# FoX's background weight work in half steps, with loads and stores a step apart from their uses

## The chip, the cores and the metric

The kernel runs on one core of one Trainium2 chip. The metric is the device time of one execution in microseconds (us). Its engines are named as in the profile: PE (TensorE matmul), PEld (its weight load), DVE (VectorE), ACT (ScalarE), POOL (GpSimd) and SP (SyncE, which issues nearly all DMAs, in order, and waits for each one's semaphores before it).

## The reference

One decoder layer on a sequence of 2048 tokens of width 1024, float32:

```python
shift_a, scale_a, gate_a, shift_m, scale_m, gate_m = split(silu(c) @ w_ada + b_ada, 6)
h = rms_norm(x, g_attn) * (1 + scale_a) + shift_a
q_f, k_f, v_f, q_s, k_s, v_s, f_logit = split(h @ w_in)
o_fox = forgetting_attention(q_f, k_f, v_f, log_sigmoid(f_logit + b))   # 8 heads, causal softmax
o_sb = stick_breaking_attention(q_s, k_s, v_s)                          # 8 heads, causal
mix = concat(head_rms_norm(o_fox, g_out_fox), head_rms_norm(o_sb, g_out_sb))
x = x + gate_a * (mix @ w_out)
h = rms_norm(x, g_mlp) * (1 + scale_m) + shift_m
u_gate, u_val = split(causal_conv3(h @ w_up))
x = x + gate_m * ((silu(u_gate) * u_val) @ w_down)
out = rms_norm(x, g_final)
```

The forgetting attention adds F[t] - F[s] to the logits, where F is the running sum of log f. c is one vector, so the six modulation vectors are one row each: gate_a and gate_m are wanted as a row that stands on all 128 partitions, shift_m and scale_m as columns.

## The kernel before

Every matmul operand is split into a high and a low part, and a product takes three matmuls. Attention is cut into 32 units: stick-breaking pairs of heads 0 to 3, then FoX pairs 0 to 3, each in four blocks of 512 tokens (tb 0 to 3). Units 16 to 31 are FoX; a unit has 6, 14, 22 or 30 groups of key tiles for tb 0 to 3. While `attend` (L596) goes through the groups of a unit, `fill_proj` puts steps of the next unit's projection between them: `proj` (L334) loads the eight tiles of h of a block from DRAM (`hp<-hs`, L339, 512 KB each), multiplies them for q, keeps them for k and, in every second pair, for v. A pair's q and k are rearranged through L285 and L295, its weights loaded at L246.

`late_mod` (L633) is work that nothing in attention needs: it hides in the FoX units. It makes the four remaining modulation vectors, parts 2 (gate_a), 5 (gate_m), 3 and 4, from eight loads of w_ada each (`hp<-in_w_ada_dram`, L654, 512 KB): ACT multiplies each half by a column of silu(c) (L660), POOL adds it to the sum `wsum` (L661). For gate_a, `fold_out` (L621) then multiplies w_out by g_out_fox and gate_a, splits the result (ACT at L44, POOL at L45) and stores it to `wos` (L631); its loads are L624. Both are generators; the main loop (L849) takes four steps of them in each of the units 17 to 30, whatever the unit's length.

One ring of ten buffers of 4 KB a partition, `h_tile()`, serves it all: the h tiles, the w_ada and w_out loads, the sums, the gate row, the folded weights. `wide()` is the same ring seen as one row:

```python
    def h_tile():
        return sl_.tile([P, 2, TB], F32R, name="hp", bufs=10)
    def wide():
        return f(h_tile()).rearrange("p a n -> p (a n)")
```

At the entry of a pair's first block (`enter_unit`, L777) all eight rows of F (`Fb<-fs`, L786: four blocks by two heads, 256 KB each) are loaded into a ring of eight that the pair before still reads (DVE at L514, POOL at L509).

The order on each engine is not the program's: a scheduler places every instruction as early as its simulated times and the free buffers let it, in-order engines then keep that order on the chip. An instruction that waits there holds all that stand behind it on its engine, SP's DMAs too.

## Time and profile before

| | before |
|---|---|
| median of 3 runs | 3091.8 us (3090.09 to 3096.59) |
| profiled execution, its own time | 3091.86 us |
| its span, first to last instruction | 3089.7 us |
| busy PE, PEld, DVE, ACT, POOL | 95%, 81%, 67%, 53%, 40% of the span |
| granted clock of PE, mean | 0.987 |
| HBM read, written | 352.61 MB, 90.51 MB |

Busy is a share of the span in which at least one instruction of the engine ran. PEclk is the granted share of the full clock: 1.00 is 2.4 GHz, 0.50 is 1.2 GHz. Stick-breaking lasts to about 850 us, FoX to about 1565 us, then come the output projection and, from about 1740 us, the channel mixer.

### The profile page before, as it was taken

Reading aid. Unit: us, or ns where it says so; the run is one execution under the profiler, and the core shown is the slowest. Engines: PE = TensorE matmul, PEld = TensorE weight load, DVE = VectorE, ACT = ScalarE, POOL = GpSimd, SP = SyncE. Lnnn points to the kernel's source line nnn. Section 1 sums busy time; section 2 is a strip of 40 time slices with the busy share of each in tenths; the row PEclk is TensorE's granted clock in tenths of the full one; section 3 lists DMA queues with packets and bytes.
Section 4 is the critical chain, followed back from the end, with each engine's and each line's share of the span. In section 5 each row is a group of like instructions: output and inputs, shape, how many; then the busy total and the mean of one; then the engine's idle time right before and its main releaser. Section 6 shows DMA issues by size and latency. Waiting matters only on the chain.

```text
span 3089.7 us, 46285 instructions
## 1 busy us (share of the span) xinstructions
PE 2945.4 (95%) x15934; PEld 2500.0 (81%) x15934; DVE 2080.9 (67%) x3416; ACT 1647.1 (53%) x3033; POOL 1228.0 (40%) x1459
## 2 busy tenths in 40 slices
PE   6899899999999999998989899999899999999998
PEld 5778798988788788987878688888678888888887
DVE  6686788878856675657733677778987777254253
ACT  5575777777765655566734544444544444343332
POOL 2673655556531332342122344444444443332331
PEclk8999999999999999999999999999999999999999
DMA  9457634565166865595457532223322223665562
GB/s 272 157 165 257 194 114 148 180 199 163 30 221 216 289 214 183 169 330 133 160 187 231 186 99 82 82 82 89 113 87 84 86 84 113 197 198 166 184 204 79
DMA packets 292811, 496.51 MB, mean 161 GB/s; under 512 B 29336, under 2 KB 177552, under 8 KB 291552
## 3 DMA queue, kind: packets, MB, share of 16 engines
q1 hardware_dynamic: 280944, 480.92, 49.4%
q10 hardware_dynamic: 11632, 12.63, 1.2%
q8 instruction: 126, 2.06, 0.3%
q14 instruction: 109, 0.89, 0.1%
HBM read 352.61 MB, written 90.51 MB: 143 GB/s over the span
## 4 chain that ended last, share of the span: by engine, by line
PE 58%; DVE 11%; DMA 10%; POOL 8%; issue 6%; ACT 4%; SPq 1%; POOLq 0%; DVEq 0%; ACTq 0%
PE ps_pj L271 8%; PE ps_o L1158 8%; PE ps_o L985 7%; PE ps_pv L401 6%; PE ps_pt L386 5%; PE ps_pj L313 5%; PE ps_t L1158 4%; PE ps_bc L1158 4%; PE ps_qk L371 3%; DMA wuraw<-in_w_up_dram 3%; PE ps_qk L372 3%; PE ps_t L985 2%; DMA hp<-hs 2%; DVE wu L45 2%; PE ps_o L738 1%
## 5 line engine op out<-in xcount | busy, mean ns | idle before, releaser
L985 PE MATMUL ps_o<-oa,wu 128*128 128x512 f32 x2088 | 503.3, 392 | 14.9 <-ACT oa L44 6.8
L985 PEld LDWEIGHTS ps_o<-oa,wu 128*128 128x128 f32 x2088 | 390.3, 188 | 105.2 <-DVE oa L45 9.8
L401 PE MATMUL ps_pv<-at,V 128*128 128x256 f32 x2304 | 432.9, 298 | 14.0 <-ACT at L390 6.0
L391 DVE TENSOR_TENSOR at<-ps_pt,at 128x512 fp32r<-128x512 f32 (+1 forms) x576 | 365.8, 653 | 117.2 <-ACT at L390 114.6
L271 PE MATMUL ps_pj<-hp,w_qk 128*128 128x512 f32 x1512 | 413.0, 405 | 28.0 <-DMA hp<-hs 13.4
L390 ACT ACTIVATE at<-ps_pt 128x512 fp32r<-128x512 f32 (+1 forms) x576 | 319.5, 580 | 169.0 <-PE ps_pt L386 126.6
L401 PEld LDWEIGHTS ps_pv<-at,V 128*128 128x128 f32 x2304 | 340.1, 191 | 48.2 <-DVE at L391 13.9
L475 POOL TENSOR_TENSOR a<-a,rw 128x512 f32<-128x512 f32 (+2 forms) x272 | 260.8, 962 | 234.8 <-DVE rw L470 98.6
L271 PEld LDWEIGHTS ps_pj<-hp,w_qk 128*128 128x128 f32 x1512 | 273.8, 190 | 86.8 <-DMA hp<-hs 17.0
L45 DVE TENSOR_TENSOR wd<-wide,wd 128x1024 fp32r<-128x1024 f32 x88 | 117.3, 1340 | 248.8 <-ACT wd L44 244.4
L371 PE MATMUL ps_qk<-K,Q 128*128 128x512 f32 (+2 forms) x640 | 257.5, 404 | 11.0 <-DMA K<-q 5.0
L45 POOL TENSOR_TENSOR g<-graw,g 128x512 fp32r<-128x512 f32 x82 | 141.3, 1726 | 294.8 <-ACT g L44 291.8
L1158 PE MATMUL ps_o<-wd,g 128*128 128x512 f32 x1040 | 249.3, 389 | 0.1
L985 PE MATMUL ps_t<-ob,wu 128*128 128x512 f32 x984 | 241.5, 390 | 0.7 <-ACT hf_m L884 0.7
L372 PE MATMUL ps_qk<-K,Q 128*128 128x512 f32 (+2 forms) x640 | 235.1, 368 | 0.0
L313 PE MATMUL ps_pj<-w_v,hp 128*128 128x256 f32 (+1 forms) x1536 | 229.9, 291 | 4.8 <-DVE zn L319 3.7
L44 ACT ACTIVATE wu<-wuraw 128x512 fp32r<-128x512 f32 x214 | 133.1, 626 | 183.4 <-PE ps_o L985 113.9
L470 DVE TENSOR_TENSOR_SCAN rw<-rw,ps_edge 128x512 f32<-128x512 f32 x168 | 211.8, 1271 | 26.1 <-ACT rw L460 25.0
L1158 PEld LDWEIGHTS ps_o<-wd,g 128*128 128x128 f32 x1040 | 195.2, 188 | 41.1 <-DVE y L1104 0.5
L985 PEld LDWEIGHTS ps_t<-ob,wu 128*128 128x128 f32 x984 | 184.7, 188 | 40.2 <-ACT hf_m L884 1.1
L313 PEld LDWEIGHTS ps_pj<-w_v,hp 128*128 128x128 f32 x1536 | 206.7, 193 | 12.9 <-issue 4.3
L386 PE MATMUL ps_pt<-edge,a 128*128 128x128 f32 x1088 | 182.3, 275 | 15.2 <-DVE at L391 8.9
(221 smaller groups left out, 5697.7 us busy)
## 6 DMA issues: line engine op xcount, KB each, us to landing
hp<-hs SPq DMA_DIRECT2D x224, 512.0 KB
wuraw<-in_w_up_dram SPq DMA_DIRECT2D x84, 512.0 KB
wide<-in_w_down_dram SPq DMA_DIRECT2D x84, 512.0 KB
Q<-q SPq DMA_DIRECT2D x128, 256.0 KB
g<-u SPq DMA_DIRECT2D x42, 512.0 KB
graw<-g SPq DMA_DIRECT2D x82, 256.0 KB
hs<-hp SPq DMA_DIRECT2D x32, 512.0 KB
K<-q SPq DMA_DIRECT2D x128, 128.0 KB
```

The lines of the kernel that those rows point to most:

```text
L45: (lo_engine or nc.gpsimd).tensor_sub(lo, src, f(hi))
L271: nc.tensor.matmul(acc, w[kt][:, a, n], h[:, bb], start=kt == 0 and i == 0, stop=kt == KT - 1 and i == 2)
L313: nc.tensor.matmul(av[:, t * width:(t + 1) * width], hts[kt][:, a, tok], w[1][kt][:, bb, 0:width], start=kt == 0 and m == 0, stop=kt == KT ...
L371: nc.tensor.matmul(b[:, :cw], Q[:, hl, 0, qcols], K[:, hl, :cw], start=True, stop=False)
L372: nc.tensor.matmul(b[:, :cw], Q[:, hl, 1, qcols], K[:, hl, :cw], start=False, stop=True)
L386: nc.tensor.transpose(b[:, i * P:(i + 1) * P], self.blk(self.kts[kk], qi), ident)
L390: nc.scalar.activation(at[:, 0, lo:], b[:, lo:], AF.Copy)
L391: nc.vector.tensor_sub(at[:, 1, lo:], b[:, lo:], f(at[:, 0, lo:]))
L401: nc.tensor.matmul(o[:, 0:2 * P], head.V[kt // 4][:, kt % 4, head.hl, :], rhs, start=self.first and kk == 0 and w == 0, stop=self.last and ...
L475: nc.gpsimd.tensor_mul(a[:, :need], a[:, :need], r[:, 1:need + 1])
L985: nc.tensor.matmul(b, w[:, p, j], o[:, q], start=first and i == 0, stop=last and i == 2, skip_group_check=True)
L1158: nc.tensor.matmul(banks[t][n], g[:, a, t * P:(t + 1) * P], w[:, b, n * TB:(n + 1) * TB], start=k == 0 and i == 0, stop=k == NKD - 1 and i ...
```

## The change

A step of the late work now handles one half row (256 KB) instead of a whole one, and 118 of them are spread evenly over the groups of units 17 to 30 (`pace`). A part's loads of w_ada all use one ring buffer `w`, whose two halves alternate: a step issues the load for the next step, then multiplies and adds its own half. The sum has a pool of its own (`late`) and also takes the gate row. `fold_out` works in place in one ring buffer; load, work and store stand in different steps, and its loads and stores are pinned behind what was issued before them on SP (`keep_in_program_order`). The rows of F are loaded block by block: blocks 0 and 1 at a pair's first unit, block 2 at its second, block 3 at its third. The instructions of PE, DVE, ACT and POOL are the same in kind and number; SP issues 64 loads of w_ada instead of 32 and 16 of w_out instead of 8.

```diff
--- before.py
+++ after.py
@@ -82,6 +82,7 @@
     mod_a = const.tile([P, 2, KT], F32, name="mod_a")
     mod_m = const.tile([P, 2, KT], F32, name="mod_m")
     bf_c = const.tile([4 * NH, 1], F32, name="bf_c")
+    LATE_STEPS = 118
     R_GA, R_GM, R_GF, R_GS, R_BA = 0, 8, 16, 20, 24
 
     def rms_scale(pool, xts, tag, junk=None):
@@ -619,17 +620,24 @@
             yield unit
 
     def fold_out(gt):
-        for kt in range(KT):
-            raw = wide()
-            nc.sync.dma_start(raw, w_out[kt * P:(kt + 1) * P, :])
-            for n in range(2):
-                sl = slice(n * TB, (n + 1) * TB)
-                nc.vector.scalar_tensor_tensor(raw[:, sl], raw[:, sl], cols[:, R_GF + kt:R_GF + kt + 1], gt[:, sl],
-                                               ALU.mult, ALU.mult)
-                w = h_tile()
-                split(w[:, 0], w[:, 1], raw[:, n * TB:(n + 1) * TB])
-                nc.sync.dma_start(wos[kt][:, :, n * TB:(n + 1) * TB], f(w))
-                yield
+        halves = [(kt, slice(n * TB, (n + 1) * TB)) for kt in range(KT) for n in range(2)]
+
+        def load(kt, sl):
+            w = h_tile()
+            tc.keep_in_program_order(nc.sync.dma_start(f(w)[:, 1], w_out[kt * P:(kt + 1) * P, sl]))
+            return w
+
+        w = load(*halves[0])
+        yield
+        for k, (kt, sl) in enumerate(halves):
+            raw = f(w)[:, 1]
+            nc.vector.scalar_tensor_tensor(raw, raw, cols[:, R_GF + kt:R_GF + kt + 1], gt[:, sl], ALU.mult, ALU.mult)
+            split(w[:, 0], w[:, 1], raw)
+            yield
+            tc.keep_in_program_order(nc.sync.dma_start(wos[kt][:, :, sl], f(w)))
+            if k + 1 < len(halves):
+                w = load(*halves[k + 1])
+            yield
 
     def late_mod():
         cr = f(h_tile())[0:2 * NFULL + 1].rearrange("p a (b n) -> p (a b) n", b=4)[:, 0:4]
@@ -648,30 +656,38 @@
         yield
         late = ((2, 0), (5, 1), (3, None), (4, None))
         for part, gate in late:
-            wsum = wide()
-            for kt in range(KT):
-                w = wide()
-                nc.sync.dma_start(w, w_ada[kt * P:(kt + 1) * P, part * D:(part + 1) * D])
-                for n in range(0, D, 512):
-                    sl = slice(n, n + 512)
-                    if kt == 0:
-                        nc.gpsimd.tensor_scalar_mul(wsum[:, sl], w[:, sl], cs[:, 0:1])
-                    else:
-                        nc.scalar.activation(w[:, sl], w[:, sl], AF.Copy, scale=cs[:, kt:kt + 1])
-                        nc.gpsimd.tensor_add(wsum[:, sl], wsum[:, sl], w[:, sl])
+            wsum = lp.tile([P, D], F32, name="wsum", bufs=1)
+            w = wide()
+
+            def load(k):
+                n = k % 2 * TB
+                nc.sync.dma_start(w[:, n:n + TB], w_ada[k // 2 * P:(k // 2 + 1) * P, part * D + n:part * D + n + TB])
+
+            load(0)
+            yield
+            for k in range(2 * KT):
+                kt, sl = k // 2, slice(k % 2 * TB, (k % 2 + 1) * TB)
+                if k + 1 < 2 * KT:
+                    load(k + 1)
+                if kt == 0:
+                    nc.gpsimd.tensor_scalar_mul(wsum[:, sl], w[:, sl], cs[:, 0:1])
+                else:
+                    nc.scalar.activation(w[:, sl], w[:, sl], AF.Copy, scale=cs[:, kt:kt + 1])
+                    nc.gpsimd.tensor_add(wsum[:, sl], wsum[:, sl], w[:, sl])
                 yield
             if gate is not None:
-                gt = wide()
-                nc.sync.dma_start(gt, b_ada[0:1, part * D:(part + 1) * D].to_broadcast([P, D]))
+                nc.sync.dma_start(w, b_ada[0:1, part * D:(part + 1) * D].to_broadcast([P, D]))
+                yield
                 for n in range(2):
+                    sl = slice(n * TB, (n + 1) * TB)
                     b = pt()
-                    nc.tensor.matmul(b, ones, wsum[:, n * 512:(n + 1) * 512], start=True, stop=True)
-                    nc.vector.tensor_add(gt[:, n * 512:(n + 1) * 512], b, gt[:, n * 512:(n + 1) * 512])
+                    nc.tensor.matmul(b, ones, wsum[:, sl], start=True, stop=True)
+                    nc.vector.tensor_add(wsum[:, sl], b, w[:, sl])
                     yield
                 if gate == 0:
-                    yield from fold_out(gt)
+                    yield from fold_out(wsum)
                 else:
-                    nc.sync.dma_start(gate_m, gt)
+                    nc.sync.dma_start(gate_m, wsum)
             else:
                 cb = pt()
                 for d in range(KT):
@@ -779,17 +795,17 @@
         while made[0] <= u.index:
             taken_before = taken[0]
             fill_proj(taken_before + 1)
-        if u.kind == "fox" and u.tb == 0:
-            Fbs[u.p] = [[sx.tile([P, TB], F32, name="Fb", bufs=8) for _ in range(NTB)] for _ in range(2)]
-            for t in range(NTB):
+        if u.kind == "fox":
+            for t in ((0, 1), (2,), (3,), ())[u.tb]:
                 for h in range(2):
-                    nc.sync.dma_start(Fbs[u.p][h][t],
-                                      fs[2 * u.p + h:2 * u.p + h + 1, t * TB:(t + 1) * TB].to_broadcast([P, TB]))
+                    b = sx.tile([P, TB], F32, name="Fb", bufs=8)
+                    nc.sync.dma_start(b, fs[2 * u.p + h:2 * u.p + h + 1, t * TB:(t + 1) * TB].to_broadcast([P, TB]))
+                    Fbs.setdefault(u.p, ([], []))[h].append(b)
         if u.index >= len(units) - 2:
             head_scale(u.index - len(units) + 2, pt(), sx)
         if u.index == len(units) - 1:
             drain(lm)
-            close_pool("sl", "psa")
+            close_pool("late", "sl", "psa")
             psc = open_pool("psc", side="right", space=PSUM)
             p2a = open_pool("p2a")
             tail = first_mix([load_o(0, p) for p in range(3)])
@@ -843,9 +859,10 @@
     ex = edge_bank = None
     psa = open_pool("psa", side="right", space=PSUM)
     sx = open_pool("fx", side="right")
+    lp = open_pool("late", side="right")
     base = taken[0]
     seen = {}
-    late = {}
+    pace = [0.0]
     for u in attend(plan[16:], 2, 2):
         seen[u.index] = seen.get(u.index, 0) + 1
         share = seen[u.index] / u.count
@@ -853,8 +870,9 @@
         if tail is not None:
             next(tail, None)
         elif u.index > 16:
-            while late.get(u.index, 0) < min(4, 4 * share):
-                late[u.index] = late.get(u.index, 0) + 1
+            pace[0] += LATE_STEPS / sum(v.count for v in plan[17:31])
+            while pace[0] >= 1:
+                pace[0] -= 1
                 next(lm, None)
     drain(tail)
     drain(first_out())
```

What the scheduler makes of it, at three places. A tile of h is named hs_k_n: k is its place among the eight, and n runs from 60 to 67 for block 0, 68 to 75 for block 1, 76 to 83 for block 2 and 84 to 91 for block 3.

SP, while gate_a is folded into w_out and pair 1 of FoX begins. Before:

```order
L786 DMA Fb<-fs 128x512 x4
L624 DMA hp<-in_w_out_dram 128x1024
L631 DMA wos_184<-hp 256x1x512
L339 DMA hp<-hs_0_76 128x1024
L295 DMA K<-q_13099 64x512 x4
L631 DMA wos_185<-hp 256x1x512
L339 DMA hp<-hs_1_77 128x1024
L624 DMA hp<-in_w_out_dram 128x1024
L786 DMA Fb<-fs 128x512
L631 DMA wos_185<-hp 256x1x512
L786 DMA Fb<-fs 128x512 x2
L339 DMA hp<-hs_2_78 128x1024
```

Now, at the same stage:

```order
L802 DMA Fb<-fs 128x512 x4
L637 DMA wos_185<-hp 256x1x512
L627 DMA hp<-in_w_out_dram 128x512
L340 DMA hp<-hs_2_70 128x1024
L340 DMA hp<-hs_3_71 128x1024
L340 DMA hp<-hs_4_72 128x1024
L340 DMA hp<-hs_5_73 128x1024
L340 DMA hp<-hs_6_74 128x1024
L340 DMA hp<-hs_7_75 128x1024
L340 DMA hp<-hs_0_76 128x1024
L340 DMA hp<-hs_1_77 128x1024
```

The tiles of block 2 stood one by one between rows of F, stores of folded weights and rearranged q and k; now the rows of F come first, and the tiles of block 1 and the first two of block 2 follow each other.

ACT, in the sum of gate_m (before at L660, now at L675), among attention's copies (L390, now L391) and exponentials (L519, now L520). Before:

```order
L660 ACTIVATE hp<-hp,cs 128x512 x2
L390 ACTIVATE at<-ps_pt 128x512
L390 ACTIVATE at<-ps_pt 128x384
L519 ACTIVATE p,ls<-p,mn 128x1792
L281 ACTIVATE q_15311<-ps_pj 128x512
L660 ACTIVATE hp<-hp,cs 128x512 x2
L390 ACTIVATE at<-ps_pt 128x512 x2
L424 ACTIVATE o_14681<-ps_pv 64x256
L390 ACTIVATE at<-ps_pt 128x512
L44 ACTIVATE q_15312<-ps_pj 128x512
L519 ACTIVATE p,ls<-p,mn 128x1920
```

Now:

```order
L675 ACTIVATE hp<-hp,cs 128x512
L391 ACTIVATE at<-ps_pt 128x512 x2
L675 ACTIVATE hp<-hp,cs 128x512
L425 ACTIVATE o_14689<-ps_pv 64x256
L391 ACTIVATE at<-ps_pt 128x512
L520 ACTIVATE p,ls<-p,mn 128x1920
L675 ACTIVATE hp<-hp,cs 128x512
L44 ACTIVATE V<-ps_pj 128x4x64
L675 ACTIVATE hp<-hp,cs 128x512
L391 ACTIVATE at<-ps_pt 128x512 x2
L44 ACTIVATE V<-ps_pj 128x4x64
```

Two halves of one load stood side by side; now they stand apart, and each has a load of its own.

SP at the end of the projections: hs_7_91 is the last tile that any projection loads. Before:

```order
L295 DMA K<-q_17794 64x512 x2
L786 DMA Fb<-fs 128x512
L339 DMA hp<-hs_7_91 128x1024
L285 DMA Q<-q_17793 64x1024
L786 DMA Fb<-fs 128x512
L285 DMA Q<-q_17793 64x1024
L786 DMA Fb<-fs 128x512
L285 DMA Q<-q_17793 64x1024 x2
L295 DMA K<-q_18154 64x512 x4
L654 DMA hp<-in_w_ada_dram 128x1024
```

Now:

```order
L340 DMA hp<-hs_7_91 128x1024
L802 DMA Fb<-fs 128x512 x4
L296 DMA K<-q_17816 64x512 x4
L802 DMA Fb<-fs 128x512
L664 DMA hp<-in_w_ada_dram 128x512
L802 DMA Fb<-fs 128x512
L664 DMA hp<-in_w_ada_dram 128x512
L286 DMA Q<-q_17815 64x1024 x3
L664 DMA hp<-in_w_ada_dram 128x512
L286 DMA Q<-q_17815 64x1024
L802 DMA Fb<-fs 128x512 x2
L664 DMA hp<-in_w_ada_dram 128x512
```

Behind the last tile one load of w_ada was left; now 14 of the last part's 16 half loads are.

## Rows read from the trace of the kernel before

**Rows 1.** The page, part 1: busy us (share), instructions of each engine, whole run.

```profile
PE 2945.4 (95%) x15934; PEld 2500.0 (81%) x15934; DVE 2080.9 (67%) x3416; ACT 1647.1 (53%) x3033; POOL 1228.0 (40%) x1459
```

**Rows 2.** Stretches: start:end, length, busy us (instructions) PE, PEld, DVE, ACT, POOL; PEclk, DMA share, GB/s.

```profile
850.00:1000.00 150.00, 148.31 (x998) 134.00 (x997) 96.83 (x286) 88.86 (x168) 43.29 (x74) 1.00 0.68 221
...
1000.00:1125.00 125.00, 113.22 (x680) 98.56 (x679) 86.35 (x240) 73.17 (x146) 43.28 (x73) 0.96 0.84 269
...
1200.00:1225.00 25.00, 20.76 (x128) 18.91 (x128) 11.12 (x34) 13.86 (x29) 6.66 (x10) 0.86 0.95 281
...
1300.00:1425.00 125.00, 119.19 (x747) 104.33 (x745) 73.19 (x203) 74.35 (x131) 48.88 (x63) 1.00 0.83 268
...
1425.00:1565.00 140.00, 131.45 (x862) 113.02 (x861) 106.81 (x311) 92.88 (x159) 24.39 (x57) 1.00 0.40 126
```

**Rows 3.** Waits of PE from 850 to 1570 us: total us, times, longest.

```profile
PE ps_pj L271 <- DMA hp<-hs: 11.1, 7, 3.9
```

**Rows 4.** Timeline of PE: start, us, merged instructions, [idle before <- what ended it].

```profile
1015.90 2.93 PE L271 MATMUL ps_pj<-hp,w_qk 128*128 128x512 f32 x6 [0.96 <-DMA hp<-hs]
...
1022.80 1.54 PE L271 MATMUL ps_pj<-hp,w_qk 128*128 128x512 f32 x6
...
1031.75 2.41 PE L271 MATMUL ps_pj<-hp,w_qk 128*128 128x512 f32 x6 [3.49 <-DMA hp<-hs]
...
1088.18 1.66 PE L271 MATMUL ps_pj<-hp,w_qk 128*128 128x512 f32 x6 [1.54 <-DMA hp<-hs]
...
1103.03 2.11 PE L271 MATMUL ps_pj<-hp,w_qk 128*128 128x512 f32 x6 [3.95 <-DMA hp<-hs]
```

**Rows 5.** Timeline of SP's queue, same columns; us runs from first to last issue.

```profile
995.60 8.36 SPq L786 DMA_DIRECT2D Fb<-fs  x4
...
1021.97 1.59 SPq L786 DMA_DIRECT2D Fb<-fs  x2
...
1071.07 9.78 SPq L246 DMA_DIRECT2D raw_qk<-in_w_in_dram  x3
```

**Rows 6.** Waits of SP's queue from 850 to 1570 us: total us, times, longest.

```profile
SPq L631 <- POOL hp L45: 25.0, 6, 12.6
...
SPq L786 <- DVE mn L514: 23.4, 14, 3.4
```

**Rows 7.** Chain of waits: DMA pieces, start and us from issue to use.

```profile
1023.61 8.10 DMA hp<-hs
...
1083.21 4.93 DMA hp<-hs
...
1201.43 9.07 DMA hp<-in_w_ada_dram
...
1382.83 7.63 DMA hp<-in_w_ada_dram
...
1582.39 2.80 DMA r<-rstd
```

**Rows 8.** Timeline of PE around 1210 us.

```profile
1213.82 1.73 PE L401 MATMUL ps_pv<-at,V 128*128 128x256 f32 x4 [3.36 <-ACT at L390]
```

**Rows 9.** Timeline of ACT around 1210 us.

```profile
1210.53 0.72 ACT L660 ACTIVATE hp<-hp,cs 128x512 f32<-128x512 f32 x1 [2.08 <-DMA hp<-in_w_ada_dram]
```

**Rows 10.** Line L654 (ada loads): count, min/median/max ns, first and last start; who waited.

```profile
L654 SPq DMA_DIRECT2D hp<-in_w_ada_dram x32: 332/341/1067, 869.4 to 1412.8; - x32
...
  ACT hp L660: 43.6, 20
```

**Rows 11.** Line L660 (ACT's multiplies): min/median/max ns, first and last start.

```profile
L660 ACT ACTIVATE hp<-hp,cs x56: 705/715/729, 899.6 to 1417.9; 128x512 f32<-128x512 f32 x56
```

**Rows 12.** Line L661 (POOL's adds): min/median/max ns, first and last start.

```profile
L661 POOL TENSOR_TENSOR hp<-hp x56: 1262/1292/1306, 900.4 to 1419.3; 128x512 f32<-128x512 f32 x56
```

## The prediction

> **What bounds the kernel now.** I began with the page: PE is busy 95% of the span [rows 1], so PE is the bound, and no instruction of PE is added or taken away. All that the change can win or lose is PE's idle time and PE's clock, and only where FoX runs, since the late work lives there. The table by stretches [rows 2] shows where that is. From 850 to 1000 us PE misses 1.7 of 150 us. From 1000 to 1125 us it misses 11.8 of 125, at a clock of 0.96; from 1200 to 1225 us 4.2 of 25, at 0.86; from 1300 to 1425 us 5.8 of 125; in the last 140 us of FoX, where no projections are left, 8.6. The clock is a loss of its own: 125 x 0.04 = 5.0 us in the second stretch and 25 x 0.14 = 3.5 us in the third.
>
> Next I asked what ends these waits. PE's largest single releaser in FoX is the load of a tile of h, 11.1 us in seven waits [rows 3]. The timeline of PE shows four of them, 0.96, 3.49, 1.54 and 3.95 us, 9.9 us together, and what follows them: six 128x512 products took 2.93 us at 1015.90 where the same six took 1.54 us at 1022.80 [rows 4]. That is the half clock (1.2 GHz), granted after the wait, and the 5.0 us of the stretch are about three such dips of 1.7 us.
>
> Then I looked at SP, because a late tile is a late issue or a slow landing. Before the 3.49 us wait, SP had spent from 995.60 to 1003.96 us on four rows of F and was at it again at 1021.97 [rows 5]; the tile went out at 1023.61 and took 8.10 us [rows 7]. In FoX the rows of F hold SP 23.4 us, waiting for DVE to be done with the old ones, and stores of folded weights hold it 25.0 us, waiting for POOL's split [rows 6]. Behind both stand loads of h: the first order listing shows it. The second pair of waits has another holder: at 1071.07 three weight loads took SP 9.78 us [rows 5], and tiles went out behind it at 1083.21 [rows 7].
>
> The wait near 1210 us is different. ACT stood 2.08 us at a multiply of the late work, for a load of w_ada that took 9.07 us [rows 7, 9]; attention's copies are queued behind it on ACT, and PE then waited 3.36 us for one [rows 8]. Such multiplies kept ACT waiting 43.6 us in 20 waits [rows 10], and this place is the only one of them that brought PE's clock down.
>
> **The change, part by part**, against the profiled execution's own 3091.86 us, which is the median (3091.8) for all purposes.
>
> *Rows of F block by block, folding in place, sums outside the ring.* Eight row loads a pair stay eight, but at a pair's entry four are wanted instead of eight; 1 MB leaves the busiest moment. In the ring a sum, a gate row and a raw row give way to one buffer, so up to nine buffers are left for h. The order shows the result: rows of F, then eight tiles and the first two of the next block in one run. What goes is the first pair of waits, 0.96 + 3.49 us, with two of the three dips, 3.3 us: 7.8 us. The second pair, 1.54 + 3.95 us with one dip of 1.7 us, 7.2 us, is held by weight loads that wait for their splits, and these stay; the stores that stood between them and the tiles now wait a step less. I take half, 3.6 us. Together 11.4 us. The bounds are 0, if other waits hold SP as long, and 15.0 us, if all four go. I see no loss here: the same bytes are moved, and later at the crowded place. What is late next is the second tile of a block: where the late sums run, the order still brings one tile early and the others behind a string of other DMAs.
>
> *Half loads, one step ahead.* A step in front came every (1417.9 - 869.4) / 56 = 9.8 us [rows 10, 11]; the halves come twice as often. They use one buffer of two halves, so a load waits for POOL's add two halves back. In 9.8 us for two halves, ACT's 0.72 and POOL's 1.29 us [rows 11, 12] leave 7.8 us for issue and landing. Whole loads took 7.63 and 9.07 us in crowded stretches; a whole tile with little around it took 4.93 us and 64 KB took 2.80 us [rows 7], so a half load lies between the last two when it is quiet. Reading between these two by size gives about 3.7 us, an estimate from two rows. So halves keep pace when it is quiet and are at the edge when it is crowded. That asks whether waiting gets more or less; I bound it from both sides. If all waits at these multiplies vanish, the one costly place gives 3.36 + 3.5 = 6.9 us. If each of the 56 multiplies waits as long as one of the 20 did, 43.6 / 20 = 2.18 us, that is 122 us; at the present price, 6.9 us of PE for 43.6 us of ACT, or 0.16, they cost 19.4 us, 12.5 more than now. I take 0, because the two pull against each other: a step of lead, but half as much data for each round trip, and the second order listing shows ACT's halves only two or three instructions apart.
>
> The Trainium skill speaks against this part: its page "DMA: Bandwidth & Descriptors", section "Anatomy of one DMA", puts a DMA at a fixed 2.0 us plus its bytes at 436 GB/s, for another way of issuing than this kernel's. By it a whole load is 3.2 us and a half 2.6 us, as an estimate, so two halves in turn cost 2 us more than one whole; the rows here agree in kind (2 x 3.7 against 4.93 us) and are slower. By its figures a half lands in far less than the 7.8 us left, even where it is crowded, so the sum would stay and the slower rival below would fall away; the rows show 9.07 us, and it keeps its chance.
>
> *40 more issues on SP.* At 0.341 us each [rows 10] they are 14 us of SP's time in some 700 us; SP is not full, and what hides them is its waiting. Cost 0; if the tiles of h were again the last thing PE waits for, they would come later by one or two issues, under 1 us at each.
>
> *Pace.* Short units get 3 half steps instead of 4 whole ones, long units 14 halves. This moves loads out of the crowded entries, counted above, and moves the end: 14 half loads now stand behind the last tile of h (third listing), where one whole load stood. That puts 14 x 0.715 = 10.0 us on ACT while attention has PE to itself, ACT is 66% and DVE 76% busy [rows 2]. It costs between +10.0 us, if all of it delays copies, and -5.8 us, the idle time of the stretch it has left. I take +1: DMA is 40% busy there, so landings are quiet, and a third of ACT is free.
>
> Sum: 3091.9 - 11.4 + 0 + 0 + 1 = 3081.5, say **3081 us**, a gain of 0.3%. A measurement of this kernel can tell about 0.2%, 6 us, from no change.
>
> **The rivals.**
>
> *Slower: the half loads set ACT's pace.* Mechanism: the add two halves back frees the half, SP issues, the half lands, ACT multiplies in its queue. It decides once landing and issue take over 7.8 us for two halves' time. For it speak 9.07 and 7.63 us [rows 7] and DMA shares of 0.95 and 0.83 where the sums run [rows 2]; against it that half loads should land sooner and that PE bore most of 43.6 us of such waits. ACT then costs 12.5 us more. SP, too, stands at each half load until POOL is through, and tiles of h are queued behind it, so the 11.4 us aren't won: 3091.9 + 12.5 + 1 = 3105 us, and 3094 us if they are won all the same.
>
> The Trainium skill's page "Perfetto Trace Analysis", section "DMA Optimizations", has this rival's condition: splitting may help when the DMA engines are generally idle, and larger transfers help where DMA is the bound. The stretches here lie on both sides of that, 0.40 and 0.95.
>
> *The waits only move.* The scheduler, not the program's steps, places the instructions. A half's multiply isn't pinned and floats to where its load lands in simulated time, so "a step apart" need not hold; and the pinned stores and loads of folding wait on SP behind whatever was issued before them. Then tiles are late elsewhere: 0 to 5 us either way, 3092 us. For it speaks that the second tile of a block is still alone in the sums; against it that the first listing is visibly cleaner.
>
> *All of it goes.* The second pair of waits too (3.6 us more) and ACT's costly wait (6.9 us): 3081.5 - 10.5 = 3071 us; with the 1 us of the end not paid and part of the 5.8 us idle from 1300 to 1425 us, some 3067 us. For it speaks that 14 of ACT's places leave the crowded stretch.
>
> **How the numbers follow.** The forecast, a gain of 4 to 17 us, has 0.48; the slower rival 0.22; waits that move 0.18; all of it 0.12. Faster by over 0.2%: 0.42 of the forecast's 0.48, 0.03 of the moving waits and the 0.12, together 0.57. Slower by over 0.2%: 0.17 of the slower rival (the rest of it, with the tiles won, is within 0.2%) and 0.03, together 0.20. Within 0.2%: 0.23. The range goes from 3067, where all is won, to 3101 us; what lies above, the slower rival's worse half, is about 0.12, and what lies below about 0.05. The forecast's own range is 3075 to 3088 us.
>
> **What would show it.** Right: PE's waits for tiles of h in FoX fall from 11.1 to under 5 us; the clock from 1000 to 1125 us is 0.98 or more; SP's waits at stores to wos nearly vanish and those at rows of F fall by half; ACT's waits at the multiplies total 30 to 65 us; the last 140 us of FoX are longer by 0 to 3 us. Wrong: ACT's waits at the multiplies over 90 us with PE waiting for copies, or SP's half loads waiting for POOL with tiles of h behind them (the slower rival); PE's waits for tiles as long as before at other places (they moved); a change of over 5 us in the stages before or after FoX, whose instructions stand as they did.

## The result: slower, and where the time went

The changed kernel takes 3118.65 us (median of 6 runs, 3110.1 to 3120.55), beside 3090.95 us of the kernel before (6 runs, 3089.59 to 3096.59): a ratio of 1.0082, 95% interval 1.0069 to 1.0094, or 25 us more by the ratio and 27.7 by the medians. Forecast were 3081 us, with 3067 to 3101 as the range. The page's part 1 for the changed kernel, which answers to [rows 1]:

```profile
PE 2965.7 (95%) x15934; PEld 2512.9 (81%) x15934; DVE 2077.0 (67%) x3416; ACT 1650.3 (53%) x3033; POOL 1226.2 (39%) x1459
```

The counts are the same. The span grew from 3089.7 to 3116.9 us, and nearly all of it in FoX. Attention's last output is stored at 1564 us in the kernel before and at 1589 us in the changed one, so that 850 to 1567 and 850 to 1592 us hold nearly the same work (4450 and 4440 matmuls). That whole stretch and the part of it up to 1200 us, with the columns of [rows 2], before:

```profile
850.00:1567.00 717.00, 683.57 (x4450) 607.35 (x4449) 470.76 (x1351) 428.38 (x791) 208.61 (x345) 0.99 0.66 209
...
850.00:1200.00 350.00, 336.54 (x2209) 302.56 (x2208) 231.93 (x657) 202.85 (x381) 102.90 (x171) 0.99 0.70 224
```

and of the changed kernel, with the stretches that answer to [rows 2] behind them:

```profile
850.00:1592.00 742.00, 694.40 (x4440) 607.41 (x4439) 467.66 (x1349) 429.69 (x789) 209.76 (x345) 0.98 0.65 202
...
850.00:1200.00 350.00, 322.13 (x2052) 281.25 (x2050) 222.83 (x640) 200.33 (x375) 106.81 (x174) 0.98 0.70 215
...
850.00:1000.00 150.00, 145.51 (x969) 129.44 (x967) 95.04 (x284) 87.48 (x166) 43.88 (x75) 1.00 0.63 191
1000.00:1125.00 125.00, 107.45 (x633) 91.09 (x634) 80.40 (x230) 67.42 (x132) 33.54 (x62) 0.96 0.78 241
1200.00:1225.00 25.00, 24.89 (x164) 22.59 (x165) 13.61 (x42) 16.72 (x33) 9.66 (x14) 1.00 0.84 282
...
1450.00:1590.00 140.00, 128.85 (x828) 110.99 (x828) 103.52 (x300) 91.65 (x158) 26.31 (x56) 0.98 0.40 128
```

FoX is 25 us longer. PE's idle time in it went from 717 - 683.6 = 33.4 to 742 - 694.4 = 47.6 us, 14.2 more; the other 11 us are a longer busy time for nearly the same matmuls. The lower clock is a part of that, some 3 us by an estimate: the sum, over stretches of 5 us, of PE's busy time multiplied by what the granted clock lacks to 1.00 is 6.8 us before and 9.6 us now. What the other 8 us are is not shown; the profile models the ends of pipelined matmuls.

All of the additional idle time lies before 1200 us: there it went from 13.5 to 27.9 us, and PE got through 2052 matmuls and not 2209. This is where gate_a is summed and folded into w_out (the folding runs from 967 to 1169 us). From 850 to 1000 us PE is idle 4.5 us where it was 1.7, from 1000 to 1125 us 17.6 us and not 11.8. Behind 1200 us the idle time is what it was, 19.7 for 19.9 us, and there a gain and a loss cancel. The wait near 1210 us is gone (24.89 of 25 us busy), as the best rival hoped; the last 140 us of FoX are idle 11.2 us and not 8.6. The longest wait there comes long after the folding, and from elsewhere:

```profile
1457.24 0.69 PE L387 MATMUL ps_pt<-edge,p 128*128 128x128 f32 x2 [3.40 <-ACT p L520]
```

ACT's exponential `p` was queued behind a split of q, which stood 4.77 us until a transfer of rows of Q, 5.84 us long, was through; the granted clock from 1440 to 1460 us was 0.81.

What ends PE's waits in FoX, beside [rows 3]:

```profile
PE ps_qk L372 <- DVE mn L515: 13.0, 16, 3.4
PE ps_pj L272 <- DMA hp<-hs: 12.4, 9, 4.4
PE ps_pt L387 <- ACT p L520: 6.0, 7, 3.4
```

The tiles of h cost as much as before. New at the top is DVE's `mn`, attention's running minimum, which stood in the kernel before with

```profile
PE ps_qk L371 <- DVE mn L514: 4.0, 6, 0.9
```

So DVE has become late, and DVE has no more to do than before. Its own waits tell why: a multiply of the folding waits for its load of w_out. In the kernel before, over the same time:

```profile
DVE hp L627 <- DMA hp<-in_w_out_dram: 3.8, 1, 3.8
```

and in the changed kernel:

```profile
DVE hp L634 <- DMA hp<-in_w_out_dram: 15.0, 8, 3.4
```

How a load comes to be late shows in the timelines of POOL, SP and DVE:

```profile
1000.74 1.29 POOL L45 TENSOR_TENSOR hp<-hp 128x512 fp32r<-128x512 f32 x1 [1.45 <-ACT hp L44]
...
1002.06 0.55 SPq L637 DMA_DIRECT2D wos<-hp  x1
1002.70 0.56 SPq L627 DMA_DIRECT2D hp<-in_w_out_dram  x1
...
1008.49 0.75 DVE L634 SCALAR_TENSOR_TENSOR hp<-hp,cols,wsum 128x512 f32<-128x512 f32 x1 [2.56 <-DMA hp<-in_w_out_dram]
```

POOL's split of a half ended at 1002.03, the store of that half (L637) left at 1002.06, the next load behind it (L627), and DVE's multiply stood 2.56 us for it. Eleven of the sixteen loads leave this way, right behind a store that leaves right behind the split. The largest of the eight waits, followed to PE, differs in one thing. The chain of waits from 1070 to 1083 us (start, us, what):

```profile
1072.56 1.01 SPq L637
...
1073.67 6.18 DMA hp<-in_w_out_dram
...
1079.88 0.03 DVE hp L634
```

Here the split had been through at 1061.19, and SP waited only 0.2 us at the store. The store itself stood behind attention's transfers on SP, an output (8.2 us of waiting for DVE) and rows of Q (5.7 us, also for DVE); the load, held behind the store, went out at 1073.67 and was of use 6.18 us later. The timelines of DVE and PE show the price:

```profile
1079.88 0.75 DVE L634 SCALAR_TENSOR_TENSOR hp<-hp,cols,wsum 128x512 f32<-128x512 f32 x1 [3.45 <-DMA hp<-in_w_out_dram]
...
1081.05 0.77 PE L372 MATMUL ps_qk<-K,Q 128*128 128x512 f32 x1 [3.45 <-DVE mn L515]
```

DVE did nothing for 3.45 us, with attention's work queued behind the one multiply; PE then stood 3.45 us for `mn`. And the clock fell after it:

```profile
1080.00:1087.00 7.00, 5.96 (x16) 4.69 (x17) 5.40 (x16) 4.28 (x8) 2.59 (x5) 0.53 0.81 265
```

A granted clock of 0.53 over 7 us is the lower level (1.2 GHz) for nearly all of them; by an estimate, 5.96 us of busy time at 0.53 hold what 3.2 us at 1.00 would, so it cost 2.8 us more.

SP's order is the other half of the story. The timeline of SP's queue, at the place of the first order listing:

```profile
1019.62 0.53 SPq L637 DMA_DIRECT2D wos<-hp  x1
1020.24 0.56 SPq L627 DMA_DIRECT2D hp<-in_w_out_dram  x1
1020.89 5.61 SPq L340 DMA_DIRECT2D hp<-hs  x8
```

The store is followed at once by the next load, as the hold demands, and the eight tiles of h that looked so clean in the listing leave in one run, late, behind a store that waited for POOL. The tile that PE wanted took 8.43 us from issue to use, and PE stood 4.4 us. SP's waits beside [rows 6] (the first two belong together, in both a store waits for POOL; so do the last two, in both a half load of w_ada does):

```profile
SPq L637 <- POOL hp L45: 18.6, 6, 14.0
SPq L637 <- POOL Fd L510: 15.7, 4, 6.5
...
SPq L802 <- DVE mn L515: 15.9, 12, 2.3
...
SPq L664 <- POOL wsum L676: 39.6, 18, 4.5
...
SPq L664 <- POOL Fd L510: 22.4, 14, 2.9
```

Rows of F hold SP for 15.9 us, a third less than the 23.4 us before. Stores hold it for 34.3 us, where they held it 25.0 us by the same releaser and 10.8 us by the other: nothing won. The half loads of w_ada (L664) hold it for 62.0 us by these two and 10.1 us by a third releaser on POOL.

ACT's multiplies wait longer [rows 10], 35 times and not 20:

```profile
ACT hp L675 <- DMA hp<-in_w_ada_dram: 68.9, 35, 5.8
```

### The profile page after: what moved, and what is told of

It is laid out like the page before. It is cut to its first block, busy times and chain, and to the rows that moved or that the text cites. A ratio compares the mean times of both kernels' runs of the same rounds, so it can differ in the third digit from the quotient of the medians.

```text
span 3116.9 us, 46359 instructions
## 1 busy us (share of the span) xinstructions
PE 2965.7 (95%) x15934; PEld 2512.9 (81%) x15934; DVE 2077.0 (67%) x3416; ACT 1650.3 (53%) x3033; POOL 1226.2 (39%) x1459
## 4 chain that ended last, share of the span: by engine, by line
PE 55%; DVE 13%; DMA 12%; POOL 8%; issue 7%; ACT 4%; SPq 1%; POOLq 0%; DVEq 0%; ACTq 0%
PE ps_pj L272 9%; PE ps_o L1176 8%; PE ps_pv L402 6%; PE ps_pt L387 5%; PE ps_pj L314 4%; PE ps_o L1003 4%; PE ps_t L1176 4%; PE ps_bc L1176 4%; DMA wuraw<-in_w_up_dram 3%; PE ps_qk L372 3%; DVE wu L45 3%; PE ps_qk L373 3%; PE ps_o L754 2%; DMA hp<-hs 2%; PE ps_t L1003 2%
## 5 line engine op out<-in xcount | busy, mean ns | idle before, releaser
L1003 PE MATMUL ps_o<-oa,wu 128*128 128x512 f32 x2088 | 504.0, 392 | 12.7 <-DVE oa L45 6.1
L272 PE MATMUL ps_pj<-hp,w_qk 128*128 128x512 f32 x1512 | 413.8, 406 | 23.5 <-DMA hp<-hs 14.5
L391 ACT ACTIVATE at<-ps_pt 128x512 fp32r<-128x512 f32 (+1 forms) x576 | 320.6, 579 | 168.5 <-PE ps_pt L387 114.5
L272 PEld LDWEIGHTS ps_pj<-hp,w_qk 128*128 128x128 f32 x1512 | 275.5, 191 | 82.5 <-DMA hp<-hs 19.7
L471 DVE TENSOR_TENSOR_SCAN rw<-rw,ps_edge 128x512 f32<-128x512 f32 x168 | 211.7, 1270 | 27.2 <-ACT rw L461 25.9
L314 PEld LDWEIGHTS ps_pj<-w_v,hp 128*128 128x128 f32 x1536 | 205.8, 193 | 11.8 <-issue 3.8
L387 PE MATMUL ps_pt<-edge,a 128*128 128x128 f32 x1088 | 182.3, 275 | 15.9 <-DVE at L392 9.2
```

The lines of the kernel that those rows point to most:

```text
L272: nc.tensor.matmul(acc, w[kt][:, a, n], h[:, bb], start=kt == 0 and i == 0, stop=kt == KT - 1 and i == 2)
L314: nc.tensor.matmul(av[:, t * width:(t + 1) * width], hts[kt][:, a, tok], w[1][kt][:, bb, 0:width], start=kt == 0 and m == 0, stop=kt == KT ...
L387: nc.tensor.transpose(b[:, i * P:(i + 1) * P], self.blk(self.kts[kk], qi), ident)
L391: nc.scalar.activation(at[:, 0, lo:], b[:, lo:], AF.Copy)
L1003: nc.tensor.matmul(b, w[:, p, j], o[:, q], start=first and i == 0, stop=last and i == 2, skip_group_check=True)
```

## The experiments

My theory after the traces: the two lines that keep w_out's loads and wos's stores in program order on SP cost most of it, because a load then waits for the store of the half before and all that this store waits for, POOL's split above all, DVE's multiply waits for the load, and attention waits for DVE. The rivals: the half loads of w_ada set ACT's pace, or the rows of F and the ring moved the tiles. Eighteen kernels, each beside the kernel before on the same chip. The next three columns are waits in FoX, in us, from the same view as above, and the last one is PE's idle time from 850 to 1200 us, all from one profiled execution of each (e6's is the fastest of its five, e8's and e9's the slowest of theirs); "holds" are the two lines of program order. The runs e1 to e4, e5 to e8, e9 to e12, e13 to e16 and e17 to e18 had a chip each, on which the kernel before took 3087.5 to 3094.29 us. Runs of different groups are compared by their ratios, and that a ratio carries from chip to chip is taken for granted.

| run | ratio to before, interval | DVE for w_out | PE for h | ACT for w_ada | PE idle to 1200 |
|---|---|---|---|---|---|
| before | 1 | 3.8 | 11.1 | 43.6 | 13.5 |
| changed kernel | 1.0082, 1.0069 to 1.0094 | 15.0 | 12.4 | 68.9 | 27.9 |
| e1 no holds | 1.0010, 1.0001 to 1.0020 | 0.8 | 3.1 | 72.0 | 11.8 |
| e2 old folding | 1.0010, 0.9999 to 1.0021 | 5.7 | 0.2 | 49.4 | 12.5 |
| e3 whole loads of w_ada | 1.0072, 1.0056 to 1.0087 | 18.2 | 13.2 | 29.7 | 22.6 |
| e4 rows of F at the entry | 1.0096, 1.0069 to 1.0123 | 9.8 | 12.6 | 65.5 | 26.9 |
| e5 only the stores held | 1.0008, 0.9994 to 1.0022 | 1.7 | 1.8 | 62.8 | 10.5 |
| e6 only the loads held | 1.0065, 1.0042 to 1.0088 | 12.7 | 10.3 | 60.9 | 21.7 |
| e7 held, load ahead of store | 1.0030, 1.0018 to 1.0042 | 5.2 | 6.8 | 62.4 | 15.2 |
| e8 no holds, whole loads of w_ada | 1.0011, 0.9998 to 1.0024 | 4.3 | 8.3 | 20.4 | 10.4 |
| e9 before + holds | 1.0036, 1.0021 to 1.0052 | 12.1 | 0.2 | 28.4 | 22.5 |
| e10 before + rows of F | 1.0005, 0.9994 to 1.0015 | 1.9 | 5.6 | 29.8 | 9.6 |
| e11 before + pace | 0.9978, 0.9966 to 0.9990 | 2.9 | 5.5 | 22.5 | 11.3 |
| e12 no holds, old pace | 1.0017, 1.0005 to 1.0028 | 0.4 | 4.5 | 49.7 | 16.1 |
| e13 pace + half loads of w_ada | 0.9989, 0.9976 to 1.0001 | 1.2 | 7.6 | 53.5 | 12.7 |
| e14 pace + folding in place | 1.0042, 1.0028 to 1.0057 | 7.1 | 7.2 | 27.2 | 15.7 |
| e15 pace + rows of F | 0.9953, 0.9938 to 0.9968 | 3.0 | 5.2 | 31.3 | 12.1 |
| e16 pace + sum's own pool | 1.0010, 0.9998 to 1.0022 | 8.3 | 10.0 | 31.4 | 15.5 |
| e17 e15 + holds | 1.0015, 1.0004 to 1.0026 | 6.9 | 4.1 | 27.1 | 15.5 |
| e18 e15 + folding in place | 1.0023, 1.0011 to 1.0035 | 8.4 | 5.6 | 32.7 | 11.9 |

### Taking one part out of the changed kernel

**e1_nopin**, both holds gone:

```diff
-            tc.keep_in_program_order(nc.sync.dma_start(f(w)[:, 1], w_out[kt * P:(kt + 1) * P, sl]))
+            nc.sync.dma_start(f(w)[:, 1], w_out[kt * P:(kt + 1) * P, sl])
-            tc.keep_in_program_order(nc.sync.dma_start(wos[kt][:, :, sl], f(w)))
+            nc.sync.dma_start(wos[kt][:, :, sl], f(w))
```

> The changed kernel without the pins on fold_out's loads and stores; all else as changed (3118.7 us). Theory: the changed kernel lost some 16 us around 1000 to 1130 us because DVE's multiply of the fold waited 15.0 us (8 times) for half loads of w_out that the pins hold behind the store before, and with it the attention work behind it on DVE. Without pins the load is free to go early: these waits fall under 5 us and the time to about 3106 us. Rival (one buffer and half the lead do it, not the pins): the waits stay at 12 us or more and the time within 4 us of 3118. Rival (the end of FoX does it all): the waits fall and the time stays.

3092.19 us beside 3090.47. Two lines carry 1.0082 - 1.0010 = 0.7%, some 22 of the 25 us. The waits of PE and of DVE's multiply (L634) in its trace:

```profile
PE ps_qk L372 <- DVE mn L515: 4.6, 10, 0.9
...
PE ps_pj L272 <- DMA hp<-hs: 3.1, 5, 1.0
...
DVE hp L634 <- DMA hp<-in_w_out_dram: 0.8, 1, 0.8
```

and the stretch up to 1200 us:

```profile
850.00:1200.00 350.00, 338.25 (x2222) 300.26 (x2221) 231.66 (x656) 210.50 (x391) 118.06 (x181) 1.00 0.76 245
```

DVE's multiply hardly waits, `mn` is back at 4.6 us, and the tiles of h, too, are on time, at 3.1 us: PE waits 8.4 us less for the one and 9.3 us less for the other, so the holds had cost it about as much through SP as through DVE. The 22 us can be found again in this one stretch. PE is idle 11.8 us in it and not 27.9, and by the same sum over 5 us as above the lower clock, which cost 5.9 us there, costs nothing: 16 + 6 = 22 us. SP shows how:

```profile
990.79 0.33 SPq L627 DMA_DIRECT2D hp<-in_w_out_dram  x1
992.15 7.30 SPq L340 DMA_DIRECT2D hp<-hs  x2
999.81 0.33 SPq L627 DMA_DIRECT2D hp<-in_w_out_dram  x1
1000.73 5.09 SPq L340 DMA_DIRECT2D hp<-hs  x2
1007.30 0.60 SPq L637 DMA_DIRECT2D wos<-hp  x1
```

The loads go out ahead of the stores, and tiles leave one or two at a time between other things. Stores wait 3.8 us for POOL and not 34.3. Here the less tidy order is the one in which PE gets its tiles in time.

**e2_oldfold**, the folding of the kernel before, which has no holds (whole-row loads, a buffer for each folded half; 100 late steps):

```diff
-            tc.keep_in_program_order(nc.sync.dma_start(f(w)[:, 1], w_out[kt * P:(kt + 1) * P, sl]))
+            raw = wide()
+            nc.sync.dma_start(raw, w_out[kt * P:(kt + 1) * P, :])
...
+                w = h_tile()
+                split(w[:, 0], w[:, 1], raw[:, n * TB:(n + 1) * TB])
+                nc.sync.dma_start(wos[kt][:, :, n * TB:(n + 1) * TB], f(w))
```

> The changed kernel with fold_out as before (whole rows from the ring, split into tiles of their own, no pins) and the pace cut to its 16 steps (100 in all). Theory: the fold's part of the loss goes, DVE waits under 5 us for w_out, PE's idle from 975 to 1225 us falls by 10 us or more, time 3102 to 3106 us; the loss of some 10 us at the end of FoX (1425 to 1475 us) stays. Rival (half loads of w_ada or the pace carry the loss): 3115 us or more.

3094.5 us, the same ratio as e1's. In this kernel, folding in place costs nothing once the holds are gone.

**e3_oldsum**, whole-row loads of w_ada from the ring (114 late steps):

```diff
-                nc.sync.dma_start(w[:, n:n + TB], w_ada[k // 2 * P:(k // 2 + 1) * P, part * D + n:part * D + n + TB])
+                w = wide()
+                nc.sync.dma_start(w, w_ada[kt * P:(kt + 1) * P, part * D:(part + 1) * D])
```

> The changed kernel with whole-row loads of w_ada from the ring again, two steps to a load; sum in its own pool, fold, pace and rows of F as changed. Theory: the loss at the end of FoX (half loads that wait for POOL on SP, ACT that waits for them, q and k late behind them) falls by half or more, the fold's loss stays: 3108 to 3112 us, ACT's waits at the multiplies from 68.9 us to under 50. Rival (the pace puts work at the end, whatever its size): ACT's waits stay over 60 us and the time within 4 us of 3118. Rival (all of the loss is the fold): 3118 with fewer ACT waits.

3112.46 us. ACT's waits at the multiplies fall from 68.9 to 29.7 us, under what they were before the change, and the time hardly moves. So the rival of the half loads is not what made this kernel slow: 39 us of ACT's waits were worth some 3 us (the intervals overlap).

**e4_oldF**, all eight rows of F at a pair's entry:

```diff
-        if u.kind == "fox":
-            for t in ((0, 1), (2,), (3,), ())[u.tb]:
+        if u.kind == "fox" and u.tb == 0:
...
+            for t in range(NTB):
```

> The changed kernel with all eight rows of F loaded at a pair's entry again. Theory: the rows of F are no part of the loss, since the scheduler issues all eight in one stretch in the changed kernel too: 3113 to 3122 us. Rival (rows asked for block by block come late and hold SP or POOL): 3110 us or less.

3123.78 us, somewhat slower than the changed kernel if at all (the intervals overlap). The new rows of F are no part of the loss.

**e5_pinstore** and **e6_pinload** take one of the two holds away each (one of e1's pairs of lines).

> The changed kernel with only the stores of folded weights pinned; the loads of w_out are free. Theory: what costs is the load that must stand behind the store before, which waits for POOL; a free load goes early, so DVE's waits for w_out fall from 15.0 us to under 6 us and the time to 3090 to 3100 us. Rival (any pin holds SP behind POOL, and tiles of h with it): DVE's waits fall, but PE's waits for tiles of h stay at 10 us or more and the time at 3108 us or more.

> The changed kernel with only the loads of w_out pinned; the stores are free. Theory: a load pinned behind what stands before it on SP in the program (the store before it, traced just ahead of it) is as late as before: DVE waits 10 us or more for w_out, 3110 us or more. Rival (the stores are what costs): 3100 us or less with DVE's waits under 8 us.

Stores held: 3092.96 us, as without any hold. Loads held: 3108.59 us, a ratio of 1.0065 and so three quarters of the cost of both holds or all of it, by its interval. In e6's waits the pattern of the changed kernel is back, though PE now meets it at another of DVE's products, `oT`:

```profile
DVE hp L634 <- DMA hp<-in_w_out_dram: 12.7, 8, 2.5
...
PE ps_pj L272 <- DMA hp<-hs: 10.3, 7, 2.7
PE ps_pv L402 <- DVE oT L426: 7.0, 4, 3.3
```

**e7_pinahead** keeps both holds, but issues the next load one step earlier, ahead of the store, into a second buffer:

```diff
+            ahead = load(*halves[k + 1]) if k + 1 < len(halves) else None
             raw = f(w)[:, 1]
...
             yield
             tc.keep_in_program_order(nc.sync.dma_start(wos[kt][:, :, sl], f(w)))
-            if k + 1 < len(halves):
-                w = load(*halves[k + 1])
+            w = ahead
```

> The changed kernel with both pins, but each load of w_out issued one step earlier, ahead of the work and the store of the half before it, into a second buffer. Theory: not the pin as such but the round trip (split on POOL, store, load, multiply on DVE) costs; with the load ahead of the store DVE's waits fall under 7 us and the time to 3092 to 3104 us. Rival (the pin as such, through SP's order): DVE's waits fall but PE waits for tiles of h 10 us or more, and the time stays over 3108 us.

3098.73 us, 1.0030. With the order turned round, DVE's waits fall from 15.0 to 5.2 us and over half of the loss goes (1.0082 to 1.0030). That the load stood behind the store of the half before is then the larger part of the cost, and that it is held at all the rest; but the second buffer came with the new order, and no run takes the two apart.

**e8_nopin_oldsum** is e1 and e3 together.

> No pins, and whole-row loads of w_ada from the ring as before (both edits of the first call that gained). Theory: PE's waits for tiles of h stay low as without pins (about 3 us against 11 in the kernel before) and ACT's waits at the multiplies fall from 72 to some 30 us, which takes back PE's extra idle time in the third pair: 3082 to 3088 us, under the kernel before. Rival (each new order of the scheduler brings waits of its own, and the total stays): 3089 to 3096 us.

3091.56 us, no better than e1 and not the gain that the theory had, with ACT's waits at 20.4 us instead of 72.0. Once more they are worth nothing that can be measured.

### Adding one part to the kernel before

**e9_beforepin** puts the two holds on the old folding:

```diff
-            nc.sync.dma_start(raw, w_out[kt * P:(kt + 1) * P, :])
+            tc.keep_in_program_order(nc.sync.dma_start(raw, w_out[kt * P:(kt + 1) * P, :]))
-                nc.sync.dma_start(wos[kt][:, :, n * TB:(n + 1) * TB], f(w))
+                tc.keep_in_program_order(nc.sync.dma_start(wos[kt][:, :, n * TB:(n + 1) * TB], f(w)))
```

> The kernel before, with its own loads of w_out and stores of folded weights held in the program's order on SP and nothing else changed. Theory (the order alone costs, wherever a load of w_out stands behind a store that waits for POOL): slower than before, 3098 to 3112 us, with DVE's waits for w_out up from 3.8 us to 8 or more. But the kernel before loads a whole row for two stores, 8 loads instead of 16, and works out of place, so its cost should lie in the lower half, about 3101. Rival (the cost needs the halves in place, one load per store): within 6 us of before, DVE's waits for w_out under 6 us.

3100.77 us beside 3087.5, as the theory had it. PE stands for what DVE and ACT make, and the tiles of h are on time (0.2 us); much of the cost is the clock, which by the sum over 5 us takes 12.4 us of FoX and not 6.8:

```profile
DVE hp L627 <- DMA hp<-in_w_out_dram: 12.1, 5, 4.4
...
PE ps_pv L401 <- DVE at L391: 7.9, 10, 3.1
PE ps_pv L401 <- ACT at L390: 6.7, 4, 3.8
```

**e10_newF** takes the loop over the rows of F from the changed kernel, **e11_pace** its even pace, with the old 59 whole steps:

```diff
-            while late.get(u.index, 0) < min(4, 4 * share):
-                late[u.index] = late.get(u.index, 0) + 1
+            pace[0] += LATE_STEPS / sum(v.count for v in plan[17:31])
+            while pace[0] >= 1:
+                pace[0] -= 1
```

> The kernel before, with the rows of F loaded block by block and nothing else changed. Theory A (the rows of F are a gain that the pinned loads hid): 3080 to 3086 us, PE's waits for tiles of h from 11.1 to under 7 us. Theory B (the rows of F come out in one stretch at a pair's entry whatever the program says, so the edit is worth nothing): 3087 to 3094 us, waits for tiles of h 9 us or more.

> The kernel before, with its 59 whole steps spread evenly over the groups of units 17 to 30 instead of four a unit. Theory (the even pace brings late work out of the pair's entry into the last long units and only moves waits): 3086 to 3096 us, less idle time of PE from 1000 to 1125 us and more after 1375 us. Rival (the even pace is what gives back the 8 us of the tiles of h): 3096 to 3103 us, with PE waiting over 8 us more after 1375 us.

The rows of F alone: PE's waits for tiles of h fall from 11.1 to 5.6 us and the time stays (1.0005): the waits are theory A's and the time theory B's. The pace alone: 3080.88 us beside 3087.5, and faster, which I had not expected at this size. Its FoX is 12 us shorter than that of the kernel before, and it loses less in PE's idle time, 705 - 681.7 = 23.3 us:

```profile
850.00:1555.00 705.00, 681.68 (x4449) 606.39 (x4449) 471.90 (x1351) 430.35 (x791) 209.19 (x345) 0.99 0.65 213
...
1000.00:1125.00 125.00, 117.86 (x719) 103.29 (x720) 86.83 (x249) 78.02 (x152) 44.52 (x76) 0.99 0.90 294
```

**e12_nopin_oldpace** is e1 with eight half steps a unit instead of the even pace.

> The changed kernel without the two holds on SP's order, and with eight half steps in each unit from 17 to 30 as the kernel before has four whole ones, instead of the even pace. If the even pace gives back after 1375 us what the tiles of h win: 3079 to 3086 us, faster than both kernels. If the half loads themselves give it back: 3088 to 3096 us, ACT's waits at the multiplies still 60 us or more.

3093.67 us: not faster, so the even pace isn't what keeps e1 from winning.

### One part beside the even pace

The pace alone is worth 0.2%, but with the other parts and no holds nothing is left of it (e1). Each part beside e11: **e13_pace_half** has the half loads of w_ada, **e14_pace_fold** the folding in place without holds, **e15_pace_F** the rows of F, **e16_pace_pool** the sum's own pool:

```diff
-            wsum = wide()
+            wsum = lp.tile([P, D], F32, name="wsum", bufs=1)
```

> The kernel before with the even pace and, beside it, only the half loads of w_ada one step ahead in one buffer; sums, gate row, folding and rows of F as before. Theory (half loads put ACT's multiplies behind loads that wait for POOL, and that is what the changed kernel's other parts give back): 3087 to 3097 us, ACT's waits at the multiplies 50 us or more against 22.5 with whole loads. Rival (the give-back lies elsewhere): within 4 us of the even pace alone (3080.9 us beside before at 3087.5).

> The kernel before with the even pace and, beside it, only the folding in place in half steps, without the two holds on SP's order. Theory (folding in place is harmless without the holds): within 4 us of the even pace alone, DVE's waits for w_out under 5 us. Rival (the 16 half loads of w_out and their 2-step round trip cost by themselves): 3086 us or more.

> The kernel before with the even pace and, beside it, only the rows of F block by block. If each edit stands for itself: 3079 to 3084 us. If the later rows of F now meet the even pace's loads in the last long units and give the gain back: 3085 to 3092 us, with PE's idle time after 1375 us up by 4 us or more.

> The kernel before with the even pace and, beside it, only the sum in a pool of its own, so that the ring has one buffer more for tiles of h. Theory: within 4 us of the even pace alone or 2 to 4 us faster, PE's waits for tiles of h at most 5.5 us. Rival (a tenth ring buffer only lets loads start earlier and collide with the rows of F): 3085 us or more.

Half loads: 3089.77 beside 3094.29 us. ACT's waits go from 22.5 to 53.5 us, as the theory had it, but the interval (0.9976 to 1.0001) overlaps that of the pace alone. Folding in place: 3105.19 us, 0.6% above the pace alone, which the theory did not have, and DVE's waits for w_out are up, from 2.9 to 7.1 us. The sum's pool: 1.0010, 0.3% above, and against the theory too; the ring has a buffer more for h, and the waits for tiles of h rise from 5.5 to 10.0 us all the same. The rows of F: 3077.43 us beside 3094.29, a ratio of 0.9953, the fastest version, by the ratio 14.5 us under the kernel before.

e11 and e15 ran on two chips, and their profiled spans are 3078.0 and 3078.5 us; that the rows of F add to the pace is likely by the ratios and not settled by the traces.

**e17_pace_F_hold** puts e9's holds on e15, **e18_pace_F_fold** the folding in place without holds.

> The fastest version so far (the kernel before with the even pace and the rows of F block by block, 0.9953 of before) and, beside it, only the two holds on SP's order at the old folding. Theory (a load of w_out held behind a store costs PE wherever it stands): 8 us or more above that version, ratio to before 0.998 to 1.003, DVE's waits for w_out from 3.0 us to 8 or more. Rival (the holds cost only in the crowded schedule of the changed kernel): ratio 0.994 to 0.997, DVE's waits for w_out under 6 us.

> The same fastest version and, beside it, only the folding in place in half steps, without the holds. If folding in place costs by itself what it cost beside the even pace alone (1.0042 against 0.9978): ratio to before 1.000 to 1.004. If that was a chance of one schedule: ratio 0.994 to 0.997.

1.0015 and 1.0023: the holds cost 0.6% there, folding in place 0.7%. The holds do it through the wait that they have in the changed kernel, though at 6.9 us, under the 8 that I had expected. e17's rows:

```profile
DVE hp L628 <- DMA hp<-in_w_out_dram: 6.9, 3, 3.5
...
PE ps_qk L372 <- DVE mn L515: 7.6, 10, 3.3
PE ps_pv L402 <- DVE at L392: 6.6, 6, 3.8
```

Folding in place does it in another way. In e18 DVE waits 8.4 us for w_out, and PE loses nothing by it: up to 1200 us it is idle 11.9 us, as in e15 (12.1), with 2234 matmuls done for 2218, and the last multiply of the folding starts at 1114 us. The loss comes later, and what brings it is not shown.

Over the whole table, PE's idle time up to 1200 us is over 21 us in five versions (the changed kernel, e3, e4, e6, e9). In all five a load of w_out is held behind the store before it, and all five stand at 1.0036 or more. e7, whose held loads stand a step earlier, has 15.2 us, and e17, held but with the pace, 15.5 us; without holds it is 9.6 to 13.5 us, but for e12, e14 and e16 (15.5 to 16.1). DVE's waits for w_out sort the runs less well: e16 has 8.3 us of them at 1.0010, e12 0.4 us at 1.0017.

## Why the prediction was wrong

**The step that failed** is "Rows of F block by block, folding in place, sums outside the ring", and in it the sentence "I see no loss here: the same bytes are moved, and later at the crowded place". I priced the folding on SP alone, as a gain, by how long stores stand before tiles of h, and gave the two holds no price there. That an instruction that waits holds all that stand behind it I applied to the store on SP and not to the multiply on DVE: load behind store, multiply behind load, attention behind multiply. On SP, too, the holds did the opposite of what I had booked: stores stood 34.3 us for POOL, with tiles of h behind them, and without the holds 3.8 us. The runs put the holds at 0.7%, some 22 us, in the changed kernel (e1), 0.4% on the kernel before (e9), 0.6% on the fastest version (e17), and most of it on the loads (1.0065 with the loads alone held in e6, 1.0008 with the stores alone in e5).

**The rivals.** The number of the slower one, 3105 us, was nearer than the forecast, but its mechanism was not what happened. Its first sign, ACT's waits over 90 us with PE behind them, did not come (68.9 us), and e3 took 39 us of such waits away for almost nothing. Its second sign came: SP stood 72.1 us at half loads until POOL was through. But e1 keeps these half loads, SP stands 75.3 us at them there, and PE waits only 3.1 us for tiles of h; so it was not this that held the tiles. "The waits only move" did name the held stores and loads behind whatever stood ahead of them, and its sign came, tiles of h as late as before (12.4 us) at other places; it had the right place, but 0 to 5 us either way is less than a quarter of the 22 us.

**Term by term.**
- *Tiles of h, -11.4 us.* In the changed kernel PE waits 12.4 us for them, not under 5. Without the holds it waits 3.1 us (e1) and with the rows of F alone 5.6 us (e10): the mechanism was right, 5.5 to 8 us of the waits go. But the time does not follow (1.0010 and 1.0005). What was wrong is to book a wait taken away as time won; other waits took its place, in e1 `PE <- ACT at L391`, 8.2 us and not 4.9.
- *Half loads, 0.* Right within the measurement (e13; e3 and e8 the same from the other side). ACT waits more, 53.5 for 22.5 us, and PE hardly hears of it. The price of 0.16 us of PE for each us of ACT's waiting was too high an upper end: e3's 39 us would have been 6 us, and came to about 3 (1.0082 to 1.0072, intervals overlapping). Two readings under this term were wrong, though the 0 did not hang on them. The 56 multiplies of [rows 11] are halves already, and the time from the first to the last holds the folding, so 9.8 us is not the time of a whole step; in the changed kernel the 56 take 875.9 to 1459.6 us, 10.4 us each on average, and not half of 9.8. And the tile of 4.93 us, read as quiet, fell in a stretch (1083 to 1088 us) with the DMA engines 0.88 busy.
- *40 more issues on SP, 0.* Not tried by itself.
- *Pace, +1.* Wrong in sign: alone it is worth -6.6 us (e11), about the -5.8 us that I had given as the end. I looked at the last 140 us, where it costs as I said (in e11 PE is idle 9.8 us there for 8.6), and not at what leaves the crowded entry: from 1000 to 1125 us PE is idle 7.1 us in e11, and was 11.8 before.
- *The signs.* The clock from 1000 to 1125 us stayed at 0.96 and did not reach 0.98. Waits at stores didn't vanish; those at rows of F fell by a third and not by half. ACT's 68.9 us lie just outside 30 to 65. Stages outside FoX stood, as said.

On the size of a half load the Trainium skill's page "DMA: Bandwidth & Descriptors", section "Anatomy of one DMA", had given 2.6 us as an estimate for 256 KB, where I read 3.7 us between two rows. The chain of the changed kernel at the start of the sums:

```profile
885.40 3.36 DMA hp<-in_w_ada_dram
...
890.97 2.74 DMA hp<-in_w_ada_dram
```

The two take 3.05 us on average, a little nearer to the page than to my 3.7 us. With the DMA engines busy neither held: the load of w_out at 1073.67 is 256 KB too and took 6.18 us, in a stretch in which the DMA share was

```profile
1072.00:1080.00 8.00, 5.53 (x36) 4.34 (x34) 4.50 (x16) 4.63 (x9) 0.59 (x2) 1.00 0.98 253
```

0.98.

**What stays open.** The parts don't add up. Folding in place costs 20 us beside the pace (e14) and 22 us beside pace and rows of F (e18), but nothing in the changed kernel without holds (e2 against e1); the sum's pool costs 10 us beside the pace (e16). Each edit gives the scheduler another order everywhere in FoX, and I have followed only the wait for w_out through it; for e14, e16 and e18 I have the totals of the table and no chain from one place to the end. A share of the differences of 0.2 to 0.4% may be such an order and not the part itself; for the holds, three kernels (e1, e9, e17) speak against that, for the pace the runs agree less (0.22% in e11, 0.07% from e12 to e1), and so for the rows of F (e4, e10, e15).
